# Compression's first layer in native float32 on four column groups of TensorE, with the norm, the values' projection and the small products around it put in another order

## The chip, the cores and the metric

The kernel runs on one NeuronCore of a Trainium2 chip. The metric is the device time of one execution in microseconds (us). Before the change it is 602.39 us, the median of three runs (601.26 to 603.01). A profile of one more execution, of 599.11 us, is what all rows below come from.

## The reference

A decoder trunk of two layers on 256 positions of width 1024, in float32.

- Layer A is an mLSTM mixer: a projection `h @ w_in` to three parts of 2048, a short convolution, gates, a chunkwise cell with four heads, and `y @ w_out` (2048 x 1024). Its result is normed and added to the residual stream `x`.
- From `x`, normed with `kv_norm`, one shared set of keys and values is computed: `kv = rmsnorm(x) @ kv_w`, six parts of 2 groups x 128. Two parts are *compressed*: blocks of 32 positions, 16 apart, get a position vector added, are flattened to 4096 values and go through `silu(flat @ w1 + b1) @ w2 + b2`; `w1` is 4096 x 256, once for keys and once for values (`kv` is 0 or 1 below). Two parts are the keys and values of a selection branch, two those of a window branch.
- Layer B is an attention mixer with 16 heads and three branches (compressed, selected, window) that read these keys and values; it has its own projections (`b_w_in`: queries, 48 branch gates, three sets of silu gates `z`) and ends in `b_w_out`, a norm, and the sum with `x`.

## The kernel before

**How a product is made.** Products are made from two halves of each operand: `hi` is the float32 value rounded to the type float32r, `lo` the rest. `split` (line 123) makes them: ScalarE (ACT) copies `src` into `hi`, VectorE (DVE) writes `lo = src - hi`. `mm3` (line 127) issues three float32r matmuls, hi*hi, hi*lo, lo*hi (lines 129 to 131 of the profile). A weight chunk is 512 KB: `weights` (line 112) issues its DMA on the queue of SyncE (SP) into one of four `raw` buffers and splits it into a ring of five `whi` and four `wlo` buffers. `proj_t` (line 136) makes one projection to 256 output columns: two chunks, 48 matmuls of 256 moving columns. A few small products take plain ("native") float32 operands; the profile shows each of these matmuls as two instructions.

**Order.** The program is traced by a layer that allots buffers, sets the waits, and orders each engine's instructions by a planner: among the instructions that its own clock says are ready it takes the earliest one of the program; `tc.high_priority()` moves instructions forward, and `tc.issue_after(ins)` queues instructions of the same engine behind `ins` without waiting for its end. `held()` does that for the list `hold`. Once made, the order on an engine or a DMA queue is fixed.

**The stretch that the change touches** (about 235 to 340 us of the span):

- `OutProj` (line 186) is layer A's output product, accumulated over 16 row tiles of `w_out`, for two tiles `t` of 128 positions and two column halves `n`. `add` runs row tiles for both `t`; `load_last` keeps the chunks of the last four row tiles (12 to 15), and `finish` runs these for `t=0`, then for `t=1`, and norms each as it ends: squares on ACT (line 161), `u` (163, DVE), a power on GpSimd (POOL, 153), a product with the norm's weights (222), the sum into `x` (224).
- Lines 552 to 574: `x` is normed with `kv_norm` (`norm_t`, line 169: product on DVE, line 175; eight transposes on TensorE (PE), line 178; a split), to `hK`. Four chunks `vch` of value weights are loaded beforehand.
- Lines 638 to 653: the values' projection `vps` for `t=0` and `t=1` (24 matmuls of 512 columns each); then `x` is normed for layer B (`hB`, both `t`).
- Lines 656 to 666: projections `xcps` of the two parts to be compressed; their hi and lo and those of the position vectors go side by side into `XC`, 68 columns per position.
- `cmp_chunk` (line 672): a chunk of `w1`, split; then four float32r matmuls (line 685), 68 stationary columns, 512 moving. Eight chunks for each `kv`, accumulated in `R` (68 x 512).
- `cmp_finish` (line 688): `R` to SBUF, four native matmuls with `comb`, which sums the parts (line 694), bias, tanh, and the second layer (line 706 for keys, 720 for values).
- `branch_gates` (line 733): 24 float32r matmuls with 48 stationary columns, a tanh, two transposes (line 751).
- Lines 896 to 908 set the order: chunks of `w1` with projections (`ks`, `kw`, gates and the first queries, three `z`) between every three chunks, `cmp_finish(0)` after the third chunk of the values, `cmp_finish(1)` last. Then the attention loop (line 917) begins with the scores `sps`.

In layer A the change touches lines 407 to 409 (`ng`, a row of running maxima) and 462 (`dps`, one native matmul per head that spreads a row of `ng` over 128 partitions).

## Time and profile before

| | |
|---|---|
| median of three runs | 602.39 us |
| profiled execution | 599.11 us, of which the span from first to last instruction is 597.3 us |
| PE busy | 580.4 us of the span (97%), granted clock 0.996 of full speed |
| DVE busy | 468.6 us (78%) |
| ACT busy | 330.6 us (55%) |
| DMA moved | 96.67 MB, mean 162 GB/s |

An engine's busy time counts its instructions; matmuls are pipelined, so the step from one matmul's start to the next, and not the duration of one, is what a matmul costs a busy PE. "PEld" is PE's loading of stationary columns. A row of a timeline gives start, duration, engine, line, operation, output and inputs, form, and how many like instructions were merged; a bracket gives the idle time of the engine before it and whom it waited for.

### The profile page before, as it was taken

Reading aid. Unit: us, or ns where it says so; the run is one execution under the profiler, and the core shown is the slowest. Engines: PE = TensorE matmul, PEld = TensorE weight load, DVE = VectorE, ACT = ScalarE, POOL = GpSimd, SP = SyncE. Lnnn points to the kernel's source line nnn. Section 1 sums busy time; section 2 is a strip of 40 time slices with the busy share of each in tenths; the row PEclk is TensorE's granted clock in tenths of the full one; section 3 lists DMA queues with packets and bytes.
Section 4 is the critical chain, followed back from the end, with each engine's and each line's share of the span. In section 5 each row is a group of like instructions: output and inputs, shape, how many; then the busy total and the mean of one; then the engine's idle time right before and its main releaser. Section 6 shows DMA issues by size and latency. Waiting matters only on the chain.

```text
span 597.3 us, 10623 instructions
## 1 busy us (share of the span) xinstructions
PE 580.4 (97%) x4002; PEld 526.2 (88%) x4002; DVE 468.6 (78%) x952; ACT 330.6 (55%) x604; POOL 91.4 (15%) x106
## 2 busy tenths in 40 slices
PE   8998999999999999899999999999999999999995
PEld 4997987989999888679778999999999999998884
DVE  5789886486888875688667688889898989899663
ACT  5565766445444344475566465747475656575621
POOL 7610000101100210250000021212121212120000
PEclk8999999999999999999999999999999999999999
DMA  9985664252421556637989654546364645354501
GB/s 256 229 261 171 213 215 138 77 171 71 142 89 55 169 180 191 186 109 226 272 261 270 184 152 132 163 123 180 111 182 117 179 114 177 108 177 142 180 32 70
DMA packets 82692, 96.67 MB, mean 162 GB/s; under 512 B 4811, under 2 KB 68449, under 8 KB 82642
## 3 DMA queue, kind: packets, MB, share of 16 engines
q1 hardware_dynamic: 81040, 92.48, 51.0%
q0 software_dynamic: 1600, 3.52, 2.7%
q8 instruction: 31, 0.51, 0.4%
q14 instruction: 19, 0.16, 0.1%
q10 hardware_dynamic: 2, 0.00, 0.0%
HBM read 94.94 MB, written 1.05 MB: 161 GB/s over the span
## 4 chain that ended last, share of the span: by engine, by line
PE 80%; DMA 7%; DVE 7%; ACT 2%; issue 2%; POOL 1%; SPq 0%; DVEq 0%; POOLq 0%; ACTq 0%
PE zps L131 10%; PE zps L129 10%; PE zps L130 10%; PE acc L129 4%; PE acc L130 4%; PE acc L131 4%; DMA raw<-in_a_w_in_dram 2%; DVE wlo L125 2%; PE qps L130 2%; PE qps L129 2%; PE qps L131 2%; PE o L129 2%; DMA raw<-in_cmp_w_dram 2%; PE o L130 2%; PE o L131 2%
## 5 line engine op out<-in xcount | busy, mean ns | idle before, releaser
L125 DVE TENSOR_TENSOR wlo<-raw,whi 128x1024 fp32r<-128x1024 f32 x169 | 204.5, 1220 | 58.2 <-ACT whi L124 17.0
L124 ACT ACTIVATE whi<-raw 128x1024 fp32r<-128x1024 f32 x169 | 176.5, 1054 | 127.6 <-issue 30.2
L129 PE MATMUL zps<-hB_hi,whi 128*128 128x256 f32 x384 | 109.3, 285 | 0.0
L131 PE MATMUL zps<-hB_hi,wlo 128*128 128x256 f32 x384 | 108.7, 283 | 0.0
L130 PE MATMUL zps<-hB_lo,whi 128*128 128x256 f32 x384 | 108.6, 283 | 0.0
L774 POOL TENSOR_SCALAR al<-dist 128x800 f32<-128x800 f32 x16 | 43.5, 2721 | 224.6 <-DVE mx L787 218.4
L129 PEld LDWEIGHTS zps<-hB_hi,whi 128*128 128x128 f32 x384 | 73.5, 191 | 0.2
L130 PEld LDWEIGHTS zps<-hB_lo,whi 128*128 128x128 f32 x384 | 73.6, 192 | 0.1
L131 PEld LDWEIGHTS zps<-hB_hi,wlo 128*128 128x128 f32 x384 | 73.6, 192 | 0.0
L795 ACT ACTIVATE e<-e,nm 128x16 f32<-128x16 f32 (+2 forms) x96 | 37.7, 394 | 12.4 <-DVE nm L790 12.0
L131 PE MATMUL xmps<-hA_hi,wlo 128*128 128x256 f32 x128 | 36.6, 286 | 3.0 <-DVE wlo L125 2.9
L129 PE MATMUL zps<-hA_hi,whi 128*128 128x256 f32 x128 | 36.6, 286 | 0.0
L129 PE MATMUL xmps<-hA_hi,whi 128*128 128x256 f32 x128 | 36.3, 284 | 0.2 <-ACT whi L124 0.2
L131 PE MATMUL zps<-hA_hi,wlo 128*128 128x256 f32 x128 | 36.4, 284 | 0.0
L130 PE MATMUL zps<-hA_lo,whi 128*128 128x256 f32 x128 | 36.3, 284 | 0.0
L130 PE MATMUL xmps<-hA_lo,whi 128*128 128x256 f32 x128 | 36.2, 283 | 0.0
L129 PE MATMUL qps<-hB_hi,whi 128*128 128x256 f32 x128 | 36.2, 283 | 0.0
L130 PE MATMUL qps<-hB_lo,whi 128*128 128x256 f32 x128 | 36.2, 283 | 0.0
L131 PE MATMUL qps<-hB_hi,wlo 128*128 128x256 f32 x128 | 36.2, 283 | 0.0
L131 PEld LDWEIGHTS xmps<-hA_hi,wlo 128*128 128x128 f32 x128 | 24.5, 192 | 3.9 <-DVE wlo L125 3.9
L129 PE MATMUL acc<-whi,yhi 128*128 128x512 f32 x64 | 25.6, 399 | 0.0
L130 PE MATMUL acc<-wlo,yhi 128*128 128x512 f32 x64 | 25.4, 397 | 0.0
(328 smaller groups left out, 1438.1 us busy)
## 6 DMA issues: line engine op xcount, KB each, us to landing
raw<-in_b_w_in_dram SPq DMA_DIRECT2D x64, 512.0 KB, 4.7
raw<-in_a_w_in_dram SPq DMA_DIRECT2D x48, 512.0 KB, 4.5
raw<-in_a_w_out_dram SPq DMA_DIRECT2D x16, 512.0 KB, 4.2
raw<-in_cmp_w_dram SPq DMA_DIRECT2D x32, 256.0 KB, 4.4
raw<-in_b_w_out_dram SPq DMA_DIRECT2D x16, 512.0 KB, 3.9
raw<-in_kv_w_dram SPq DMA_DIRECT2D x8, 512.0 KB, 5.5
raw<-in_kv_w_dram SPq DMA_DIRECT2D x8, 256.0 KB, 4.3
x<-in_x_dram SPq DMA_DIRECT2D x4, 256.0 KB, 3.8
```

Source lines behind the costliest of these rows:

```text
L124: a = nc.scalar.activation(hi, src, AF.Copy)
L125: return a.ins, nc.vector.tensor_sub(lo, src, hi.bitcast(F32)).ins
L129: nc.tensor.matmul(dst, lhsT=l[0], rhs=r[0], start=start, stop=False)
L130: nc.tensor.matmul(dst, lhsT=l[0], rhs=r[1], start=False, stop=False)
L131: last_mm[0] = nc.tensor.matmul(dst, lhsT=l[1], rhs=r[0], start=False, stop=stop).ins
L774: nc.gpsimd.tensor_scalar(al, dist, -slopes[h], None, op0=ALU.mult)
L795: nc.scalar.activation(e[:, c0:c0 + n], e[:, c0:c0 + n], AF.Exp, bias=nm[:, i:i + 1], accum_out=sm[:, i:i + 1])
```

## The change

- `finish` runs the matmuls of both `t` first and norms afterwards; layer A's last part has six row tiles in place of four. The chunks of the added two row tiles are split into four of the large `h8` buffers ("homes"), not into the ring.
- The norm for `hK` is traced at high priority and queued on PE behind a matmul three before the end of the output product. The values' projection of each `t` comes right behind its norm, and the norm for `hB` behind that.
- The first layer of the compression is native: `XC` is plain float32 with the position vectors added, 32 columns for each half `a` of a block, and the chunk of `w1` is used as loaded. A chunk is four native matmuls of 32 stationary and 256 moving columns, each into another quarter of the 128 rows of `R`. `w1` has nine buffers of its own (six, and three that take the place of the value weights); nine chunks are asked for while `XC` is made, the others one by one as chunks are used.
- `cmp_finish` is cut in two: `cmp_hidden` (two native matmuls) and the rest; both are queued behind the last matmul of a projection. The list of calls is written out anew.
- The branch gates' hi and lo stand side by side (96 columns): 16 matmuls in place of 24, and two native matmuls in place of the transposes, before the tanh.
- `dps` becomes one float32r matmul of 36 rows, on a hi and lo of `ng` that DVE makes.

```diff
-    def weights(src, a):
+    def weights(src, a, home=None):
...
-        hi = wp.tile([P, 1024], F32R, tag="whi", bufs=5, name=f"whi{n}")
-        lo = wp.tile([P, 1024], F32R, tag="wlo", name=f"wlo{n}")
+        if home is not None:
+            hi, lo = home[:, 0, :], home[:, 1, :]
+        else:
...
         def one(self, t, n, k, wt):
...
+                if kk == 0:
+                    self.near_end = last_mm[0]
...
-        def load_last(self, k0):
-            self.last = [(n, k, self.load(n, k)) for n in range(2) for k in range(k0, self.nk, 2)]
+        def load_last(self, k0, spare=0):
+            homes = [[hp.tile([P, 2, 1024], F32R, tag="h8", name=f"wl{n}{k}") for n in range(2)] for k in range(0, spare, 2)]
+            self.last = [(n, k, self.load(n, k, homes[(k - k0) // 2][n] if k < k0 + spare else None))
+                         for k in range(k0, self.nk, 2) for n in range(2)]
+            self.last.sort(key=lambda e: e[0])
...
             for t in range(NT):
                 for n, k, wt in self.last:
                     self.one(t, n, k, wt)
+            for t in range(NT):
                 with tc.high_priority(), held():
...
+        ng2 = ap.tile([36, S], F32R, name="ng2")
+        pick2 = ap.tile([36, AH], F32R, name="pick2")
+        for t in (ng2, pick2):
+            nc.vector.memset(t.bitcast(F32), 0.0)
+        for r in (0, 32):
+            nc.vector.tensor_copy(pick2[r:r + AH], ident[r:r + AH, r:r + AH])
...
+        nc.vector.tensor_copy(ng2[0:AH], ng)
+        nc.vector.tensor_sub(ng2[32:32 + AH], ng, ng2[0:AH].bitcast(F32))
...
-            nc.tensor.matmul(dps, lhsT=ident[0:AH, h:h + 1].to_broadcast([AH, P]), rhs=ng, start=True, stop=True)
+            nc.tensor.matmul(dps, lhsT=pick2[:, h:h + 1].to_broadcast([36, P]), rhs=ng2, start=True, stop=True)
...
-        op.add(4, (AH - 1) * HT)
-        op.load_last((AH - 1) * HT)
+        op.add(4, (AH - 1) * HT - 2)
+        op.load_last((AH - 1) * HT - 2, 2)
...
-            ins = norm_t(t, rB[t], gam_k, hK)
+            with tc.high_priority(), tc.issue_after(op.near_end):
+                ins = norm_t(t, rB[t], gam_k, hK)
...
+            vps.append(pjt([P, 512], f"vps{t}"))
+            if t == 0:
+                op_end = last_mm[0]
+            with tc.issue_after(op_end):
+                for c in range(4):
+                    for k in range(2):
+                        kk = 2 * c + k
+                        mm3(vps[t], [a[:, kk, t * P:(t + 1) * P] for a in hK], [a[:, k, :] for a in vch[c]],
+                            kk == 0, kk == KT - 1)
+            if t == 0:
+                hB = new_hT("hB")
+            with tc.issue_after(last_mm[0]):
+                norm_t(t, rB[t], gam_b, hB)
...
-        comb = kp.tile([68, 2, BG, NB], F32, name="comb")
+        comb = kp.tile([P, BG, NB], F32, name="comb")
...
+        w1p = [cctx.enter_context(tc.tile_pool(name="w1p", bufs=6, reuse_waits="tile"))]
+        w1t = []
+        def load_w1(eng):
+            i = len(w1t)
+            kv, c = divmod(i, 8)
+            src = cmp_w1[kv].rearrange("(a l p) n -> p l a n", a=2, p=P)
+            raw = w1p[i % 9 // 6].tile([P, 2, 2, 256], F32, tag="w1", name=f"w1_{i}")
+            for l in range(2):
+                eng.dma_start(out=raw[:, l], in_=src[:, 2 * c + l])
+            w1t.append(raw)
...
-        b2 = bctx.enter_context(tc.tile_pool(name="b2", bufs=2, side="right", reuse_waits="tile"))
-        pp = bctx.enter_context(tc.tile_pool(name="pp", bufs=7, side="right", reuse_waits="tile"))
-        hB = new_hT("hB")
-        for t in range(NT):
-            norm_t(t, rB[t], gam_b, hB)
+        qz = bctx.enter_context(tc.tile_pool(name="qz", bufs=2, side="right", reuse_waits="tile"))
+        w1p.append(cctx.enter_context(tc.tile_pool(name="w1q", bufs=3, side="right", reuse_waits="tile")))
...
             hold.clear()
-            X = kp.tile([P, 16, 68], F32R, tag=f"XC{kv}", name=f"XC{kv}")
+            for _ in range((6, 3)[kv]):
+                load_w1(nc.sync)
+            X = kp.tile([P, 2, 16, 32], F32, tag=f"XC{kv}", name=f"XC{kv}")
             psv = ps.rearrange("p g (c l) -> p g c l", l=16)
-            xh, xl = (X[:, :, o:o + 32].rearrange("p l (g c) -> p g c l", g=BG) for o in (0, 32))
-            split(xh, xl, psv)
-            pos = cvec[:, kv * 32:(kv + 1) * 32].rearrange("p (a l) -> p l a", a=2)
-            split(X[:, :, 64:66], X[:, :, 66:68], pos)
+            for a in range(2):
+                pos = cvec[:, kv * 32 + a * 16:kv * 32 + (a + 1) * 16]
+                nc.vector.tensor_add(X[:, a].rearrange("p l (g c) -> p g c l", g=BG), psv,
+                                     pos[:, None, None, :].to_broadcast([P, BG, 16, 16]))
...
         def cmp_chunk(kv, c, R):
...
-            split(hi, lo, raw)
-            for l in range(2):
-                for i, w in enumerate((hi, lo)):
-                    nc.tensor.matmul(R, lhsT=XC[kv][:, 2 * c + l, :], rhs=w[:, l * 512:(l + 1) * 512],
-                                     start=c == 0 and l == 0 and i == 0, stop=c == 7 and l == 1 and i == 1)
+            raw = w1t[kv * 8 + c]
+            for l in range(2):
+                for a in range(2):
+                    r = 32 * (2 * l + a)
+                    nc.tensor.matmul(R[r:r + 32, :], lhsT=XC[kv][:, a, 2 * c + l, :], rhs=raw[:, l, a, :],
+                                     start=c == 0, stop=c == 7)
+            if len(w1t) < 16:
+                load_w1(nc.sync)
+
+        def cmp_hidden(kv, R):
+            rs = tp.tile([P, 256], F32, tag="tmp", name="rs")
+            nc.scalar.activation(rs, R, AF.Copy)
             ps = wkt([P, 2, BG * NB], "hidps")
+            with tc.issue_after(last_mm[0]):
+                for ht in range(2):
+                    nc.tensor.matmul(ps[:, ht, :], lhsT=rs[:, ht * P:(ht + 1) * P],
+                                     rhs=comb.rearrange("p g n -> p (g n)"), start=True, stop=True)
...
             for k in range(KT):
-                mm3(ps, [a[:, k * NGL:(k + 1) * NGL] for a in (hi, lo)], [a[:, k, :] for a in hB], k == 0, k == KT - 1)
-            gT = tp.tile([NGL, S], F32, tag="tmp", name="gT")
-            nc.scalar.activation(gT, ps, AF.Tanh, scale=0.5)
+                for i in range(2):
+                    nc.tensor.matmul(ps, lhsT=hl[:, k].rearrange("p i c -> p (i c)"), rhs=hB[i][:, k, :],
+                                     start=k + i == 0, stop=k + i == KT)
+            gT = tp.tile([2 * NGL, S], F32, tag="tmp", name="gT")
+            nc.scalar.activation(gT, ps, AF.Copy)
...
             for t in range(NT):
-                nc.tensor.transpose(gps[:, t, :], gT[:, t * P:(t + 1) * P], ident[0:NGL, 0:NGL])
-            nc.vector.tensor_scalar(gs, gps, 1.0, 0.25, op0=ALU.add, op1=ALU.mult)
+                nc.tensor.matmul(gps[:, t, :], lhsT=gT[:, t * P:(t + 1) * P], rhs=both_parts, start=True, stop=True)
+            nc.scalar.activation(gs, gps, AF.Tanh, scale=0.5)
+            nc.vector.tensor_scalar(gs, gs, 1.0, 0.25, op0=ALU.add, op1=ALU.mult)
...
+        ks()
+        chunks(0, 0, 4)
+        kw()
+        chunks(0, 4, 8)
+        gT = branch_gates()
+        put(q, 0, q_proj, 0)
+        gate_columns(gT)
+        h0 = cmp_hidden(0, Rs[0])
+        chunks(1, 0, 3)
+        z0[0]()
+        cmp_finish(0, *h0)
+        chunks(1, 3, 8)
+        z0[1]()
+        h1 = cmp_hidden(1, Rs[1])
+        z0[2]()
+        cmp_finish(1, *h1)
         cctx.close()
+        b2 = bctx.enter_context(tc.tile_pool(name="b2", bufs=2, side="right", reuse_waits="tile"))
+        pp = bctx.enter_context(tc.tile_pool(name="pp", bufs=7, side="right", reuse_waits="tile"))
```

The silu gates and the queries move from the pools `pp` and `b2` to `qz`; `chunks(kv, c0, c1)` calls `cmp_chunk` for these chunks.

## Rows read from the trace of the kernel before

**Rows 1.** The profile's page: busy time of the engines over the span, share and number of instructions; and the splits of weight chunks, count, busy time, mean ns of one, and idle time before them.

```profile
PE 580.4 (97%) x4002; PEld 526.2 (88%) x4002; DVE 468.6 (78%) x952; ACT 330.6 (55%) x604; POOL 91.4 (15%) x106
...
L125 DVE TENSOR_TENSOR wlo<-raw,whi 128x1024 fp32r<-128x1024 f32 x169 | 204.5, 1220 | 58.2 <-ACT whi L124 17.0
L124 ACT ACTIVATE whi<-raw 128x1024 fp32r<-128x1024 f32 x169 | 176.5, 1054 | 127.6 <-issue 30.2
```

**Rows 2.** Busy time in stretches of 10 us: length, then busy time (instructions) of each engine, granted clock, mean busy share of the DMA engines, GB/s.

```profile
260.00:270.00 10.00, 10.00 (x70) 9.10 (x69) 9.65 (x15) 6.42 (x11) 4.76 (x2) 1.00 0.34 107
...
280.00:290.00 10.00, 10.00 (x73) 8.83 (x71) 6.24 (x7) 5.12 (x6) 0.00 (x0) 1.00 0.91 283
```

**Rows 3.** Timeline of PE: the end of layer A's output product, the norm for `hK` and the values' projection, up to the first `xcps`.

```profile
246.79 0.40 PE L131 MATMUL acc<-whi,ylo 128*128 128x512 f32 x1
248.88 0.66 PE L178 MATMUL nT<-ident,nrm 128*128 128x128 f32 x4 [1.70 <-DVE nrm L175]
...
250.57 0.40 PE L129 MATMUL vps<-wvhi,hK_hi 128*128 128x512 f32 x1
...
255.84 0.39 PE L131 MATMUL vps<-wvhi,hK_lo 128*128 128x512 f32 x1
256.96 1.29 PE L178 MATMUL nT<-ident,nrm 128*128 128x128 f32 x8 [0.74 <-DVE nrm L175]
258.28 0.50 PE L129 MATMUL vps<-wvhi,hK_hi 128*128 128x512 f32 x1
...
264.29 1.91 PE L178 MATMUL nT<-ident,nrm 128*128 128x128 f32 x16
265.95 0.36 PE L129 MATMUL xcps<-hK_hi,whi 128*128 128x256 f32 x1
```

**Rows 4.** Timeline of PE: the first three chunks of the first layer (line 685, 12 matmuls from 277.55) and the projection behind them; then the two places with a wait for `wlo`.

```profile
277.55 0.40 PE L685 MATMUL R<-whi,XC 128*68 128x512 f32 x1
...
280.30 0.28 PE L129 MATMUL ksps<-hK_hi,whi 128*128 128x256 f32 x1
...
290.97 0.38 PE L131 MATMUL kwps<-hK_hi,wlo 128*128 128x256 f32 x1 [0.32 <-DVE wlo L125]
...
299.03 0.39 PE L685 MATMUL R<-whi,XC 128*68 128x512 f32 x1
300.19 0.45 PE L685 MATMUL R<-wlo,XC 128*68 128x512 f32 x1 [0.77 <-DVE wlo L125]
```

**Rows 5.** Timeline of PE in layer A: the gates' product `gps` (line 377), 32 native matmuls of 32 stationary and 256 moving columns on the four quarters in turn, shown as 64 instructions (first and last two groups), with what stands behind; and eight instructions (four native matmuls of 256 columns) on the whole array, line 472, up to the next group.

```profile
86.71 0.64 PE L377 MATMUL gps<-xm,wgt 128*32 128x256 f32 x8
...
89.33 0.61 PE L377 MATMUL gps<-xm,wgt 128*32 128x256 f32 x8
89.76 0.61 PE L377 MATMUL gps<-xc,wgt 128*32 128x256 f32 x8
90.30 0.39 PE L129 MATMUL zps<-hA_hi,whi 128*128 128x256 f32 x1
...
138.70 0.69 PE L462 MATMUL dps<-ng,ident 4*128 4x256 f32 x2
139.32 1.99 PE L472 MATMUL sps<-xc,kk 128*128 128x256 f32 x8
141.15 1.05 PE L474 MATMUL sps<-xc,kk 128*128 128x128 f32 x8
```

**Rows 6.** Timeline of PE: branch gates (24 matmuls from 300.93), the gates' transposes, the small product behind the first layer, and the second layer of the keys.

```profile
300.93 0.28 PE L129 MATMUL bgps<-hB_hi,whi 128*48 128x256 f32 x1
...
303.93 0.28 PE L129 MATMUL qps<-hB_hi,whi 128*128 128x256 f32 x1
...
309.76 0.32 PE L751 MATMUL gTps<-ident,gT 48*128 48x48 f32 x2
310.01 1.08 PE L694 MATMUL hidps<-comb,rs 68*128 68x32 f32 x8
310.92 0.43 PE L685 MATMUL R<-whi,XC 128*68 128x512 f32 x1
...
314.56 0.28 PE L130 MATMUL zps<-hB_lo,whi 128*128 128x256 f32 x1
316.31 0.63 PE L706 MATMUL kcps<-hid,w 128*128 128x32 f32 x4 [1.48 <-DVE hid L703]
...
339.09 0.37 PE L129 MATMUL sps<-KThi,qhi 128*128 128x272 f32 x1
```

**Rows 7.** Layer A: DVE's chain at `ng`, and PE's transposes of `grows` behind it.

```profile
98.92 0.28 DVE L409 TENSOR_SCALAR ng<-ng 4x256 f32<-4x256 f32 x1
99.24 0.41 DVE L411 TENSOR_TENSOR grows<-ng,grows 4x256 f32<-4x256 f32 x1
...
99.86 0.58 PE L420 MATMUL tps<-ident,grows 4*128 4x4 f32 x4
```

**Rows 8.** Queues: SP's issues of weights before and behind the norm (start, time from the first to the end of the last of so many issues); two issues of POOL, of which the first is of line 914 (through the helper in line 65) and the second of line 588.

```profile
237.92 6.61 SPq L116 DMA_DIRECT2D raw<-in_kv_w_dram  x4
262.10 8.18 SPq L679 DMA_DIRECT2D raw<-in_cmp_w_dram  x6
...
255.99 0.62 POOL L65 DMA_DIRECT2D gam_o<-in_norm_post_dram  x1
256.61 0.55 POOL L588 DMA_DIRECT2D crows<-in_cmp_pos_dram  x1
```

More of the change, by code (lines that the diff above doesn't have):

```diff
@@ L116, in weights @@
         nc.sync.dma_start(out=raw.rearrange("p (a b) -> p a b", a=a), in_=src)
-        hi = wp.tile([P, 1024], F32R, tag="whi", bufs=5, name=f"whi{n}")
-        lo = wp.tile([P, 1024], F32R, tag="wlo", name=f"wlo{n}")
+        if home is not None:
+            hi, lo = home[:, 0, :], home[:, 1, :]
+        else:
+            hi = wp.tile([P, 1024], F32R, tag="whi", bufs=5, name=f"whi{n}")
+            lo = wp.tile([P, 1024], F32R, tag="wlo", name=f"wlo{n}")
         with held():
@@ L192, in __init__, with load @@
             self.acc = [[(wkt if t + n == 2 else pjt)([P, 512], f"acc{t}{n}") for n in range(2)] for t in range(NT)]
-        def load(self, n, k):
-            return weights(self.w[k * P:(k + 2) * P, n * 512:(n + 1) * 512].rearrange("(k p) n -> p k n", p=P), 2)
+        def load(self, n, k, home=None):
+            return weights(self.w[k * P:(k + 2) * P, n * 512:(n + 1) * 512].rearrange("(k p) n -> p k n", p=P), 2, home)
         def one(self, t, n, k, wt):
@@ L565, in trunk @@
         hK = new_hT("hK")
-        rB = []
+        rB, vps = [], []
         for t, n in op.finish():
@@ L639, in trunk @@
         for t in range(NT):
-            ps = pjt([P, 2, BG * DK], f"vps{t}")
-            for c in range(4):
-                for k in range(2):
-                    kk = 2 * c + k
-                    mm3(ps.rearrange("p a b -> p (a b)"), [a[:, kk, t * P:(t + 1) * P] for a in hK],
-                        [a[:, k, :] for a in vch[c]], kk == 0, kk == KT - 1)
-            split(V[t][0], V[t][1], ps)
-        vctx.close()
-        b2 = bctx.enter_context(tc.tile_pool(name="b2", bufs=2, side="right", reuse_waits="tile"))
@@ L701, in cmp_finish @@
             nc.scalar.activation(th, hid, AF.Tanh, scale=0.5)
+            return hid, th
+        def cmp_finish(kv, hid, th):
             if kv == 0:
@@ L704, in cmp_finish @@
                 kps = wkt([P, BG * NB], "kcps")
-                for ht in range(2):
-                    nc.tensor.matmul(kps, lhsT=w2[:, 0, ht, :], rhs=hid[:, ht, :], start=ht == 0, stop=ht == 1)
+                with tc.issue_after(last_mm[0]):
+                    for ht in range(2):
+                        nc.tensor.matmul(kps, lhsT=w2[:, 0, ht, :], rhs=hid[:, ht, :], start=ht == 0, stop=ht == 1)
                 kc = kp.tile([P, BG, NB], F32, name="kc")
@@ L719, in cmp_finish @@
                                                        op0=ALU.add, op1=ALU.mult)
-                        nc.tensor.matmul(vps[:, g, :], lhsT=l.rearrange("p r n -> p (r n)"), rhs=w2[:, 1, ht, :], start=ht == 0, stop=ht == 1)
+                        with tc.issue_after(last_mm[0]):
+                            nc.tensor.matmul(vps[:, g, :], lhsT=l.rearrange("p r n -> p (r n)"), rhs=w2[:, 1, ht, :], start=ht == 0, stop=ht == 1)
                 vcf = tp.tile([6 * NB, BG, DK], F32, tag="tmp", name="vcf")
@@ L737, in branch_gates @@
                               in_=bw[:, NQK:NQK + NGL].rearrange("(k p) c -> p k c", p=P))
[L738 to L741 removed]
+            hl = wp.tile([P, 1024], F32R, tag="whi", bufs=5, name=f"whi{n}")[:, 0:2 * KT * NGL].rearrange(
+                "p (k i c) -> p k i c", k=KT, i=2)
+            split(hl[:, :, 0, :], hl[:, :, 1, :], raw.rearrange("p (k c) -> p k c", k=KT))
+            ps = pjt([2 * NGL, S], "bgps")
             for k in range(KT):
[L743 to L746 removed]
+                for i in range(2):
[3 more added lines that the diff above has]
+            nc.scalar.activation(gT, ps, AF.Copy)
+            return gT
+        both_parts = bp.tile([2 * NGL, NGL], F32, name="both_parts")
+        nc.gpsimd.tensor_add(both_parts, ident[0:2 * NGL, 0:NGL], ident[0:2 * NGL, NGL:2 * NGL])
         def gate_columns(gT):
@@ L759, in q_proj @@
             ps = proj_t(bw, p * 256, hB, "qps")
-            q = [b2.tile([P, 2, S], F32R, tag=f"q{s}", name=f"q{s}{p}") for s in ("hi", "lo")]
+            q = [qz.tile([P, 2, S], F32R, tag=f"q{s}", name=f"q{s}{p}") for s in ("hi", "lo")]
             sc = float(DK) ** -0.5
```

58 lines of the change are left out of this document (14 added, 44 removed).

## The prediction

> **What bounds the kernel now.** I read the page first: PE is busy 97% of the span, no other engine over 78% [rows 1]. So I ask what the change takes from PE's path, matmul by matmul, and what makes PE wait in its place. I then read PE's timeline by steps from one start to the next, and set each excess over the usual step down as a wait. In layer A's end PE stands still twice, for the norm's chain [rows 3]. Behind it the first layer of the compression runs at its own step, with short waits for `wlo`, which DVE makes [rows 4]. One longer wait is the keys' second layer, queued inside a projection before its input is there [rows 6]. Last I read the stretches for DVE and DMA, the candidates for a new bound: DVE is full (9.65 of 10 us) while the norms run, with DMA at 0.34; later DMA is at 0.91 and 283 GB/s [rows 2].
>
> **The first layer.** Now 12 matmuls take 280.30 - 277.55 = 2.75 us, 0.229 each, so 64 take 14.7 us [rows 4]. After: 16 chunks of four native matmuls of 32 x 256. The gates' product in layer A has just this form: eight instructions, that is four matmuls on four quarters, step by 0.43 us (89.33 to 89.76) [rows 5]. 16 x 0.43 = 6.9 us: **-7.8**. The full-array row, eight instructions in 141.15 - 139.32 = 1.83 us, is the other bound: 64 matmuls at 0.46 would be 29.3 us, **+14.6**. I take 0.43, since form, types and order over the quarters are the same; the far end is a rival.
>
> Leaving such a burst costs 0.54 - 0.43 = 0.1 us [rows 5]; with as much for entering, four bursts cost **+0.8**, between 0 and 1.6. The Trainium skill, page "TensorEngine Tiling (Array Packing)", section Tiling Modes, says that changing the tiling mode drains the TensorE. The row agrees that a change costs something, and shows that it is small.
>
> The 16 splits go (1.22 us of DVE and 1.05 of ACT each [rows 1], 20 and 17 us). Both engines are off the path, so that alone gives nothing on PE; it gives the waits for `wlo`: 300.19 - 299.03 - 0.23 = 0.93 in the chunks and 0.32 in `kwps` [rows 4]: **-1.25**, between 0 and -1.6. In place of two splits of `xcps` per part come two DVE additions, hidden by the next projections; without that cover they would cost about as much as the splits that they replace. POOL's `comb` has fewer pieces, and is long done.
>
> **Small products.** Gates: 24 matmuls take 3.00 us, 0.125 each; 16 take 2.0: **-1.0**. The two transposes cost 0.25; two native matmuls are four instructions, at hidden's 0.91/8 = 0.11 about 0.46: **+0.2**. The hidden product goes from eight instructions to four, twice: 2 x 0.91/2, **-0.9**. The keys' second layer waits 316.31 - 314.56 - 0.12 = 1.6 us for `hid`; after, three chunks and a whole projection lie in between: **-1.6** [rows 6]. Tanh and scaling of the gates on ACT and DVE are hidden until the first softmax needs them.
>
> **The norm's stretch.** PE loses 2.09 - 0.23 = 1.86 us before the first transposes of `hK`, 1.12 - 0.23 = 0.89 before the second ones, 0.5 inside these (8 in 1.32 us, where 16 later take 1.66), and 0.5 in the second `vps` (6.01 us; the first took 5.5) [rows 3]: 3.7 us. After, `t=1` runs 36 matmuls instead of 24 while `t=0` is normed: 12 x 0.23 = 2.8 us more cover than the 1.86 that is short. For the second gap, eight transposes of `hB` (0.83 us) lie in the queue ahead. But these need a product on DVE, between the chain's own DVE steps, and DVE is full there [rows 2]. Bounds: 0, if DVE delays the chain by what the order gains, and -3.7. I take **-2.8**, nearer to the rows of PE, since the larger gap has a margin of 0.9 us. What is late next is the split of the first `xcps` chunk. The homes of the two added row tiles lie in buffers that layer A's projections left long before, so they wait for nothing; the DMAs are as many as before.
>
> **`dps`.** Two instructions take 139.32 - 138.70 = 0.62 us, four times [rows 5]. One float32r matmul of 256 columns steps by 0.12 to 0.2: 4 x 0.47, **-1.9**; bounds -1.6 and -2.0. DVE gets a copy and a subtraction on four rows, like those of 0.28 and 0.41 us, ahead of the step that ACT and then PE's transposes `tps` wait for [rows 7]; the memsets can run earlier. If nothing stands ready ahead of `tps` on PE, this costs up to 0.7: **+0.4**, between 0 and 0.8.
>
> **Loads.** A 512 KB chunk takes 0.524 MB / 283 GB/s = 1.85 us [rows 2]. From the end of the output product to the scores, 28 such chunks are needed (16 of `w1`, 4 for `ks` and `kw`, 8 for the queries and three `z`): 52 us. That stretch is 339.09 - 250.57 = 88.5 us now [rows 3, 6] and some 74 after, so DMA suffices on average. It is better used: SP issued nothing between 244.5 and 262.1 [rows 8], and six buffers of `w1` come free when the output product ends. Some loads may still come late (the three buffers in the place of the value weights; the loads 9 to 15, each behind its chunk). Bounds 0 and two loads late, 3.7; I take **+0.85**, nearer to the waits that rows show today.
>
> **Sum.** -7.8 + 0.8 - 1.25 - 1.0 + 0.2 - 0.9 - 1.6 - 2.8 - 1.9 + 0.4 + 0.85 = **-15.0 us**. Against the profiled execution, 599.11, that is 584.1. That execution lies 3.3 us under the median of 602.39, and a measurement will give a median: **587.4 us**. Nothing behind the scores changes but the place of some buffers.
>
> **Rivals.**
> *Loads in the program's order* (slower). If SP's queue keeps the order in which the code asks, four loads of `w1`, the first waiting for the first chunk, stand ahead of `kw`'s weights. From that chunk's end: four loads and one of `kw`, 5 x 1.85, and its split, 1.05 + 1.22, are 11.5 us, less three chunks of 0.43: PE waits 10.2. Then three loads and the first of the queries, 7.4 us (the gates' small one left out), and a split, less 1.3: another 8.4. Together 18.6: 606.0. It turns slower once loads cost 15 us. For it: a queue's order is fixed, and SP stood still once for 17 us. Against: POOL's queue sent a load of line 914 ahead of one of line 588 [rows 8], so what is ready goes first. 0.06.
> *Quarters that overlap less*, the change not doing what it says. At 0.46 each, 29.3 - 6.9 = 22.4 more: 609.8. With an overlap of three a chunk takes 1.83 / 3 = 0.61 us, 16 x 0.18 = 2.9 more: 590.3. The Trainium skill, page "TensorE: Matmul & The Clock Gate", section "Measured speedup vs the span model", gives 3.07 times for four row tiles, by an estimate 0.60 us a chunk. Against both: 64 instructions in 3.59 us, and 1.83 / 0.43 = 4.3 times [rows 5]. 0.04, nearly all for the milder form.
> *DVE holds the norm*: the -2.8 is not there, and the first `xcps` waits for its split, 1.2 us: 591.4. For it: 9.65 of 10 us busy [rows 2]. Against: PE's larger gap lacks 1.86 us of cover and gets 2.8 [rows 3]. 0.15.
> *Late loads*: 3.7 and a split of 2.3 in place of 0.85: 592.5. For it: 0.91 of DMA [rows 2]. Against: the longer lead. 0.10.
>
> **How the numbers follow.** My forecast has 0.65. With every term at its good end (-7.8, 0, -1.6, -1.0, +0.2, -0.9, -1.6, -3.7, -2.0, 0, 0) the sum is -18.4, 584.0; runs spread by 1.1 us under their median and some waits are perhaps longer than I count, so the range begins at 581.5. At the other end the two faster rivals together give 596.5; I stop at 595. About 0.1 is left above (loads in order, both rivals at once, serial quarters) and 0.07 below. Within 0.3% (1.8 us, about what a measurement can tell from no change) lies only a mixture of losses of 13 to 17 us: 0.02. Slower is most of the first rival and the serial quarters: 0.06. Faster: 0.92.
>
> **What would show it.** Right: `R` in bursts of 16 to 20 matmuls, 0.43 us per chunk, some 8 us of PE fewer; DVE with 16 splits fewer; no idle PE before the transposes of `hK`; `kcps` without a wait; `dps` one instruction each; scores starting near 324. Wrong: PE waiting for `whi` or `wlo` of `kwps`, `bgps` or `qps`, with SP's queue waiting for a matmul of line `R` (loads in order); a chunk above 0.6 us; `xcps` waiting for DVE; or a stretch from the scores to the end longer than today's 258 us, which I did not count at all.

## The result and the profile after

The kernel takes **585.23 us** (median of four runs, 584.39 to 585.7) against 601.83 (four runs, 600.24 to 603.01): ratio 0.973, 95% interval 0.971 to 0.976. The forecast was 587.4, in a range of 581.5 to 595.0. The profiled execution took 585.10 us, span 583.3; before, 599.11 and 597.3.

First the page after: busy time of the engines, and the splits of weight chunks.

```profile
PE 571.7 (98%) x4048; PEld 520.5 (89%) x4048; DVE 450.0 (77%) x942; ACT 311.4 (53%) x585; POOL 89.5 (15%) x103
...
L128 DVE TENSOR_TENSOR wlo<-raw,whi 128x1024 fp32r<-128x1024 f32 x150 | 181.4, 1221 | 61.3 <-PE zps L134 22.1
L127 ACT ACTIVATE whi<-raw 128x1024 fp32r<-128x1024 f32 x151 | 157.2, 1053 | 122.1 <-issue 26.4
```

Against [rows 1], DVE and ACT each lose 19 us of work, and that is more than the span lost; yet only 14 us of span went, because PE bounds, before and after. So the comparison goes by PE's landmarks, the first start of a group. PE starts the projections of layer A at 16.4 us after and at 14.5 before, with the same work ahead of it; over the 13 kernels profiled below and here this start lies between 13.8 and 16.5 us. It is a spread between executions. From the gates' product `gps` on, stretches in which nothing was changed repeat within 0.3 us over these kernels, most of them within 0.05, so I count from there; a difference under 0.3 us in one stretch says nothing by itself.

| from, to (us) | before | after | difference |
|---|---|---|---|
| `gps` to first `acc` (with `dps`) | 115.26 | 114.25 | -1.01 |
| `acc` to `vps` | 48.60 | 46.80 | -1.80 |
| `vps` to `xcps` | 15.38 | 14.78 | -0.60 |
| `xcps` to scores (first layer, gates) | 73.14 | 58.60 | -14.54 |
| scores to last `acc` | 251.46 | 254.11 | +2.65 |
| whole | 503.84 | 488.54 | **-15.30** |

In the profile after, `gps` starts at 87.99, the first `acc` at 202.24, the scores at 322.42 and the last `acc` at 576.53 us.

The stretch from the scores on isn't a loss, though it is longer. Before, 164 matmuls of `zps` ran ahead of the scores, 20 of them of the next part; after, 144 do. The 20, at 0.12 us, are 2.4 us that moved behind the scores. So the last of the prediction's signs of being wrong, a stretch from the scores to the end longer than 258 us, is there (260.9), but as moved work; the stretch ahead of the scores is shorter by the same 2.4.

The norm's stretch (compare [rows 3]):

```profile
247.47 1.03 PE L181 MATMUL nT<-ident,nrm 128*128 128x128 f32 x8
...
248.81 0.39 PE L134 MATMUL acc<-whi,ylo 128*128 128x512 f32 x1
249.04 0.40 PE L132 MATMUL vps<-wvhi,hK_hi 128*128 128x512 f32 x1
...
254.60 2.33 PE L181 MATMUL nT<-ident,nrm 128*128 128x128 f32 x15
...
257.80 0.50 PE L134 MATMUL vps<-wvhi,hK_lo 128*128 128x512 f32 x1 [0.21 <-DVE hK_lo L128]
...
263.82 0.37 PE L132 MATMUL xcps<-hK_hi,whi 128*128 128x256 f32 x1
```

No transpose has a bracket now; the eight of `t=0` lie inside layer A's last products, those of `t=1` run with seven of `hB` in one row of 15. Of PE's waits in the whole stretch, 0.21 us is left.

The first layer and the small products (compare [rows 4, 6]), the last three of four bursts of `R`, each with the group behind it, the small products between, and the scores:

```profile
289.09 1.93 PE L712 MATMUL R<-w,XC 128*32 128x256 f32 x32
290.95 0.36 PE L778 MATMUL bgps<-hB_hi,whi 128*96 128x256 f32 x1
...
292.91 0.28 PE L132 MATMUL qps<-hB_hi,whi 128*128 128x256 f32 x1
...
299.03 0.60 PE L723 MATMUL hidps<-comb,rs 128*128 128x32 f32 x4
299.56 1.50 PE L712 MATMUL R<-w,XC 128*32 128x256 f32 x24
300.99 0.38 PE L132 MATMUL zps<-hB_hi,whi 128*128 128x256 f32 x1
...
306.84 0.53 PE L739 MATMUL kcps<-hid,w 128*128 128x32 f32 x4
307.29 2.37 PE L712 MATMUL R<-w,XC 128*32 128x256 f32 x40
309.59 0.39 PE L132 MATMUL zps<-hB_hi,whi 128*128 128x256 f32 x1
...
322.42 0.37 PE L132 MATMUL sps<-KThi,qhi 128*128 128x272 f32 x1
```

The four bursts last 1.87, 1.86, 1.43 and 2.30 us (four, four, three, five chunks), 7.46 in all: 0.435 for a chunk more, and 0.13 for entering and leaving. Gates took 1.96 us, the hidden product 0.53, and `kcps` starts with no wait.

SP's queue after (compare [rows 8]) holds what one rival was about:

```profile
249.23 6.75 SPq L677 DMA_DIRECT2D w<-in_cmp_w_dram  x12
261.46 0.37 SPq L116 DMA_DIRECT2D raw<-in_kv_w_dram  x1
261.93 3.01 SPq L677 DMA_DIRECT2D w<-in_cmp_w_dram  x6
265.04 4.14 SPq L116 DMA_DIRECT2D raw<-in_kv_w_dram  x3
270.09 0.48 SPq L770 DMA_DIRECT2D raw<-in_b_w_in_dram  x1
...
281.97 5.70 SPq L677 DMA_DIRECT2D w<-in_cmp_w_dram  x8
```

Nine chunks of `w1` (two issues each) go out early, and the weights of `ks`, `kw`, gates and queries stand *ahead* of the loads that wait for a chunk to be used. The program asks for them behind. The two stretches of [rows 2], after:

```profile
260.00:270.00 10.00, 10.00 (x74) 9.45 (x73) 7.99 (x11) 4.27 (x6) 0.00 (x0) 1.00 0.92 289
...
280.00:290.00 10.00, 10.00 (x112) 8.46 (x114) 5.29 (x7) 4.67 (x6) 0.00 (x0) 1.00 0.97 290
```

In the first, DVE falls from 9.65 to 7.99 us and DMA rises from 107 to 289 GB/s: the loads now use the time in which SP had stood still.

### The profile page after: what moved, and what is told of

Its sections match the earlier page's. It is cut to its first block, busy times and chain, and to the rows that moved or that the text cites. A ratio compares the mean times of both kernels' runs of the same rounds, so it can differ in the third digit from the quotient of the medians.

```text
span 583.3 us, 10621 instructions
## 1 busy us (share of the span) xinstructions
PE 571.7 (98%) x4048; PEld 520.5 (89%) x4048; DVE 450.0 (77%) x942; ACT 311.4 (53%) x585; POOL 89.5 (15%) x103
## 4 chain that ended last, share of the span: by engine, by line
PE 94%; DVE 3%; issue 1%; ACT 1%; POOL 0%; DVEq 0%; POOLq 0%; ACTq 0%
PE zps L132 11%; PE zps L134 11%; PE zps L133 11%; PE acc L132 5%; PE acc L134 5%; PE acc L133 5%; PE qps L133 3%; PE qps L132 3%; PE qps L134 3%; PE o L132 2%; PE o L133 2%; PE o L134 2%; PE xmps L134 2%; PE xmps L133 2%; PE xmps L132 2%; PE pt L860 2%
## 5 line engine op out<-in xcount | busy, mean ns | idle before, releaser
L128 DVE TENSOR_TENSOR wlo<-raw,whi 128x1024 fp32r<-128x1024 f32 x150 | 181.4, 1221 | 61.3 <-PE zps L134 22.1
L127 ACT ACTIVATE whi<-raw 128x1024 fp32r<-128x1024 f32 x151 | 157.2, 1053 | 122.1 <-issue 26.4
L132 PE MATMUL o<-whi,hA_hi 128*128 128x512 f32 x64 | 25.3, 396 | 0.0
L132 PEld LDWEIGHTS xmps<-hA_hi,whi 128*128 128x128 f32 x128 | 24.5, 192 | 0.9 <-ACT whi L127 0.6
```

What stands on the lines that cost most here:

```text
L127: a = nc.scalar.activation(hi, src, AF.Copy)
L128: return a.ins, nc.vector.tensor_sub(lo, src, hi.bitcast(F32)).ins
L132: nc.tensor.matmul(dst, lhsT=l[0], rhs=r[0], start=start, stop=False)
```

## The experiments

Times are medians; "shift" is the difference to the profile after from `gps` to the last `acc`, which leaves the start out. All edits are to the changed kernel unless said.

**The start.** The kernel before, unchanged, for a second profile.

> The kernel before, unchanged, profiled once more. The two profiles at hand differ at their start: the first xmps matmul stands at 14.45 us before and at 16.38 us after, though the change has nothing there. Theory (the start's spread): the first xmps of this second profile lies anywhere from 14 to 17 us, and from the first xmps to the first scores sps it repeats the 324.6 us of the first profile within 1.5 us. Rival (the change moves the start, by the memsets of ng2 and pick2 and by another instruction stream): 14.45 us again within 0.2.

That execution took 1456.85 us, with PE busy for 1445.9 of it: an outlier that says nothing of the start. The spread of the start is read from the other profiles instead.

**1. Quarters one at a time.** In each burst all chunks of one column group, then those of the next.

```diff
-            for c in range(c0, c1):
-                cmp_chunk(kv, c, Rs[kv])
+            for quarter in range(4):
+                for c in range(c0, c1):
+                    cmp_chunk(kv, c, Rs[kv], quarter)
```

> The kernel after, but within a burst of chunks the matmuls of one quarter of R follow each other (all chunks for quarter 0, then 1, 2, 3); same matmuls, same result, same loads. Theory (quarters run beside each other only when successive matmuls lie in different quarters): a native matmul on its own steps by 0.43 to 0.46 us, so 64 take 27.5 to 29.3 us instead of 7.4, and the kernel is 20 to 22 us longer, 605 to 607 us. Rival (the 32-column form is cheap by itself, whatever the order): within 1.5 us of 585.2. Between: overlap only at the changes of quarter, 64 - 16 steps of 0.43 and little else, still 15 us longer or more.

595.54 us (594.58 to 596.52), shift +10.7, all of it in `R`: 18.09 us in place of 7.46. Neither size was met. The bursts, PE's timeline:

```profile
305.53 2.87 PE L711 MATMUL R<-w,XC 128*32 128x256 f32 x24
308.33 0.39 PE L132 MATMUL zps<-hB_hi,whi 128*128 128x256 f32 x1
...
314.63 6.32 PE L711 MATMUL R<-w,XC 128*32 128x256 f32 x40
320.88 0.38 PE L132 MATMUL zps<-hB_hi,whi 128*128 128x256 f32 x1
```

Twelve matmuls took 2.80 us, 16 took 4.52 twice, 20 took 6.25. That is 0.43 for each one more. My mean of 0.28, on which I built the next expectation, was the wrong reading: the bursts aren't proportional to their length, they are 0.43 per matmul less a fixed 2.4 us, which is what the three changes of group in a burst overlap. The starts of the single instructions agree: the 40 of the last burst fall into four series at 0.216 us an instruction, and each series begins 1.33 us behind the start of the one before. Ten instructions need 2.16 us, so each series overlaps the one before by 0.83.

**2. Two groups in turn.** One pair of groups for all chunks of a burst, then the other pair.

```diff
+            for half in range(2):
+                for c in range(c0, c1):
+                    for quarter in (2 * half, 2 * half + 1):
+                        cmp_chunk(kv, c, Rs[kv], quarter)
```

> As the changed kernel, but in each burst the matmuls alternate between two of the four column groups, first one pair for all its chunks, then the other. In the run with one group at a time a matmul took 0.28 us, with four in turn 0.11. Theory (each group takes 0.28 us for its own matmul and groups overlap whole): 0.14 us per matmul, 2.3 us for a burst of 16 and 9.2 us for all 64, 587 us. Rival A (two neighbours don't overlap, or only in part): 0.2 to 0.28 us, 13 to 18 us in all, 591 to 595. Rival B (two groups are enough and something else sets 0.11): 7.5 us, 585.2.

588.86 us (two runs), shift +3.8; `R` took 11.02 us, between the theory's 9.2 and rival A's 13.

```profile
301.36 1.96 PE L711 MATMUL R<-w,XC 128*32 128x256 f32 x24
303.25 0.39 PE L132 MATMUL zps<-hB_hi,whi 128*128 128x256 f32 x1
...
309.56 3.68 PE L711 MATMUL R<-w,XC 128*32 128x256 f32 x40
313.18 0.39 PE L132 MATMUL zps<-hB_hi,whi 128*128 128x256 f32 x1
```

1.89, 2.76 and 3.62 us for 12, 16 and 20 matmuls: 0.216 for each one more. With one group in turn it is 0.43, with two 0.216, with four 0.109. So the theory's mechanism holds, at 0.43 and not at 0.28: a group needs 0.43 us for its matmul, and groups that alternate overlap whole. The Trainium skill, page "TensorEngine Tiling (Array Packing)", section Tiling Modes, says that different tiles can execute in parallel; these three steps agree.

**3. The native layer alone.** The kernel *before* with the native first layer, its weights through the four `raw` buffers that all weights share, and nothing else of the change.

```diff
-            hi = wp.tile([P, 1024], F32R, tag="whi", ...)
-            lo = wp.tile([P, 1024], F32R, tag="wlo", ...)
-            split(hi, lo, raw)
...
-                    nc.tensor.matmul(R, lhsT=XC[kv][:, 2 * c + l, :], rhs=w[:, l * 512:(l + 1) * 512], ...)
+                    r = 32 * (2 * l + a)
+                    nc.tensor.matmul(R[r:r + 32, :], lhsT=XC[kv][:, a, 2 * c + l, :], rhs=rv[:, l, a, :], ...)
```

> The kernel before with the native first layer on four quarters alone: chunks in the four raw buffers, used as loaded, the old order of calls, four-tile end, old values, gates and dps. Theory (the first layer's own PE time is most of the gain): chunks fall from 14.7 to 7.4 us, the hidden product by 0.9, and the wait for wlo in the chunks goes: 8.5 to 9.5 us less than before, 592.3 to 593.3 us. Rival (the buffers of w1 are needed: a raw buffer is now held until its matmuls, so loads come later): new waits of PE for DMA of 2 to 6 us in the stretch of the chunks, 594 to 599 us.

611.39 us (608.85 to 613.67) against 600.01 of the kernel before: 1.9% longer (ratio 1.019, 1.015 to 1.022), and outside both ranges. PE waited 4.6 us for `w1` and 3.8 for the splits of `kw` and the gates; the granted clock was 0.83 in 290 to 310 us.

**4. The shared buffers in the new order.** That run also had the old order of chunks and projections. So the changed kernel, in its order, with `w1` through the four `raw` buffers:

```diff
-            raw = w1p[i % 9 // 6].tile([P, 2, 2, 256], F32, tag="w1", ...)
+            raw = wp.tile([P, 1024], F32, tag="raw", ...)
...
-            for _ in range((6, 3)[kv]):
-                load_w1(nc.sync)
```

> As the changed kernel, in its order, but the first layer's weights go through the four buffers that all raw weights share, as in the kernel before, and nothing is loaded ahead. Theory (a native matmul holds its raw buffer until PE is through with it, where a split on ACT and DVE let go of it earlier; so the shared buffers stop the loads of the projections behind them): PE waits 8 to 20 us ahead of chunks and projections, 593 to 605 us. Rival (the slow run with the native layer alone came from chunks and projections being interleaved three by three, not from the buffers): waits under 3 us, 585 to 588.

611.81 us (610.85 to 612.59), shift +26.7: the shared buffers without a lead do it, in the new order too; the loss is larger than I allowed. The waits named add up to 14 us; the granted clock falls to 0.66 behind them, and PE's steps get longer. PE's waits (us in total, times, longest) and one of SP, then a stretch (length, busy time of PE, PEld, DVE, ACT and POOL, granted clock, DMA share, GB/s):

```profile
PE zps L132 <- ACT whi L127: 4.5, 1, 4.5
...
PE kwps L132 <- ACT whi L127: 3.5, 1, 3.5
PE R L710 <- DMA raw<-in_cmp_w_dram: 2.9, 1, 2.9
PE bgps L774 <- DVE whi L128: 2.9, 1, 2.9
```

```profile
SPq L116 <- PE R L710: 19.3, 8, 7.9
```

The row of SP shows the mechanism: SP's issues of the projections' weights (line 116) stood 19.3 us behind matmuls of `R`. In the profiles before and after, no issue of that line waits for `R`. The stretch:

```profile
300.00:310.00 10.00, 8.37 (x44) 8.06 (x45) 3.13 (x4) 3.32 (x6) 0.00 (x0) 0.66 0.96 268
```

**5. A short ring of its own.** Four buffers for `w1` in place of nine, four loads ahead.

```diff
-        w1p = [cctx.enter_context(tc.tile_pool(name="w1p", bufs=6, ...))]
+        w1p = [cctx.enter_context(tc.tile_pool(name="w1p", bufs=4, ...))]
...
-        w1p.append(cctx.enter_context(tc.tile_pool(name="w1q", bufs=3, ...)))
...
-            for _ in range((6, 3)[kv]):
+            for _ in range((4, 0)[kv]):
```

> As the changed kernel, but the first layer's weights have four buffers in place of nine, and only four chunks are issued ahead of the compression's projections; the next is issued when a chunk has been used, as the other loads are. Theory A (the lead of the loads is what the new buffers bring, and without it the native chunks wait, as in the run with the native layer alone, where two waits were 3.0 and 2.8 us): chunks 4 to 15 wait, 3 to 8 us in all, 588 to 593 us. Theory B (the chunks spread behind projections give enough time, and in the native layer alone it was the planner's interleaving that cost): 585.2 +- 1 us, bursts of 7.5 us in all.

588.03 us (586.83 to 589.21), shift +3.7, at the lower end of theory A's range: the second burst took 293.18 - 289.45 = 3.73 us in place of 1.86, `R` 10.01 in all. That is 2.6 us more, a little under the 3 to 8 that theory A named; another 0.9 lies in `zps`, between whose matmuls the last chunks came singly. PE's timeline:

```profile
289.45 3.80 PE L711 MATMUL R<-w,XC 128*32 128x256 f32 x32
293.18 0.36 PE L777 MATMUL bgps<-hB_hi,whi 128*96 128x256 f32 x1
```

So a lead of four chunks in place of nine costs under 4 of run 4's 26.7 us; the rest is left for the ring that the projections' weights share, and for loading nothing ahead. These two were not tried apart.

**6. Loads in the program's order.** The weights of `ks`, `kw`, the gates and the first queries are issued behind the loads of `w1` that the program has ahead of them.

```diff
-        kw()
+        with tc.issue_after(last_ld[0]):
+            kw()
```

(and the same for `ks`, and for the gates with the queries)

> As the changed kernel, but the weights of ks, kw, the gates and the first q projection are issued on SP only after the loads of the first layer's weights that stand ahead of them in the program: nine chunks ahead of ks, four more ahead of kw, the rest ahead of the gates. In the profile after, the planner had put the weights of kw, the gates and part of q ahead of the last seven chunks. Theory (that order is why PE waits for no load there): a chunk is 512 KB, 1.6 us at the 323 GB/s of that stretch, so ks comes about 3 x 1.6 = 5 us later than its need, kw and the gates up to 7 x 1.6 = 11 us: 590 to 600 us, and the profile shows PE waits of 1 us and more ahead of ksps, kwps or bgps. Rival (the buffers for raw weights lead by enough to cover it): 585.2 +- 1 us and no wait over 0.3 us ahead of those projections.

598.14 us (596.44 to 600.56), shift +14.2, in the theory's range. Its wait came ahead of `kw` alone: ahead of `ks` and the gates' product PE waited for no load. SP's queue, then PE's timeline, then one stretch:

```profile
283.52 3.95 SPq L678 DMA_DIRECT2D w<-in_cmp_w_dram  x8
287.56 1.37 SPq L116 DMA_DIRECT2D raw<-in_kv_w_dram  x2
```

```profile
296.19 0.58 PE L132 MATMUL kwps<-hK_hi,whi 128*128 128x256 f32 x1 [9.71 <-ACT whi L127]
...
299.11 0.41 PE L132 MATMUL kwps<-hK_hi,whi 128*128 128x256 f32 x1
299.32 0.41 PE L133 MATMUL kwps<-hK_lo,whi 128*128 128x256 f32 x1
```

```profile
290.00:300.00 10.00, 3.35 (x14) 3.05 (x15) 2.45 (x2) 2.11 (x2) 0.00 (x0) 0.50 1.10 334
```

The weights of `kw` went out at 287.56 in place of 265.04, behind the loads that wait for the first burst, and PE stood for 9.71 us, close to the 10.2 that the prediction's rival gave for this wait. That rival's second wait, 8.4 us ahead of the queries, did not come. Behind the wait a matmul stepped by 0.21 us where it takes 0.12: the granted clock is 0.50 in this stretch, the lower of the two levels (1.2 GHz), after PE had stood still. From the first `kwps` to `bgps` it is 9.42 us, in the profile after 5.95 without the burst that lies there: 3.5 us more, of which 0.5 is a second wait and the rest the clock.

**7. Small products at once.** Hidden product and second layer right behind the chunks, no forced order.

```diff
-        h0 = cmp_hidden(0, Rs[0])
         chunks(1, 0, 3)
+        cmp_finish(0, *cmp_hidden(0, Rs[0]))
```

(and the same for the second compression; the three `tc.issue_after(last_mm[0])` around these small products go)

> As the changed kernel, but the second layer of the compression follows its hidden product at once, right behind the chunks, with nothing issued between and no order forced. Theory (the wait of 1.63 us ahead of kcps was the chain hidden product, addition, tanh, product on DVE and ACT, and placing projections between took it away): the wait of about 1.6 us comes back for the first compression, and one of the same chain ahead of the second's values product, where no projection is left to cover it: +1.6 to +3.2 us, 586.8 to 588.4. Rival (the planner moves the small products back by itself, or fills the wait with matmuls that are ready): +0 to +0.5 us.

587.49 us (586.2 to 589.1), shift +1.7: the theory's lower end.

```profile
303.62 0.63 PE L739 MATMUL kcps<-hid,w 128*128 128x32 f32 x4 [1.55 <-DVE hid L735]
```

The first wait is back. In place of the second, the planner ran 21 `zps` of the next part ahead of the scores, as the kernel before did: `ksps` to scores is 4.43 us longer, scores to the end 2.73 shorter.

**8. Four row tiles at the end.**

```diff
-        op.add(4, (AH - 1) * HT - 2)
-        op.load_last((AH - 1) * HT - 2, 2)
+        op.add(4, (AH - 1) * HT)
+        op.load_last((AH - 1) * HT)
```

> The kernel after, with four row tiles in the last part of the output product as before, the rest as changed. Theory (the two added row tiles give the cover for the norm of t=0): PE stands still again before the first transposes of hK, by 1.2 to 2.0 us; 586.4 to 587.4 us. Rival (the order with high priority and near_end gives the gain): no idle time of PE there beyond 0.3 us, within 0.4 us of 585.2.

588.0 us (586.92 to 588.77), shift +3.5, all of it between `acc` and `vps`; more than the theory's 1.2 to 2.0, of its sign. PE's timeline, the first transposes and the first `vps`; then the same stretch in this run and in the kernel before:

```profile
250.18 0.85 PE L181 MATMUL nT<-ident,nrm 128*128 128x128 f32 x4 [2.19 <-DVE nrm L178]
...
252.97 0.63 PE L132 MATMUL vps<-wvhi,hK_hi 128*128 128x512 f32 x1
```

```profile
245.00:255.00 10.00, 7.81 (x31) 6.14 (x30) 7.74 (x15) 4.01 (x10) 4.41 (x10) 0.83 0.42 126
```

```profile
245.00:255.00 10.00, 8.30 (x41) 6.44 (x40) 6.86 (x12) 5.27 (x14) 4.69 (x12) 1.00 0.36 105
```

The wait explains some 2 us, and the granted clock behind it, 0.83, the rest. From the first transposes to the first `vps` eleven matmuls take 252.97 - 250.18 = 2.79 us here and 250.57 - 248.88 = 1.69 in the kernel before [rows 3], at a clock of 1.00; with the next three `vps`, 1.13 us where the kernel before takes 0.72, the clock cost about 1.5 us of this execution. Without it the shift would be some 2.0, the theory's upper end. Two of the other executions took 586.92 and 587.31 us at a mean clock of 0.999 and 0.998, in the theory's range; the third took 588.77 at 0.997. In run 3 a wait of 2.13 us at the same place left the clock at 1.00.

**9. Values behind both norms.** The values' projection of both `t` after both `t` of the first norm, as before.

```diff
-            with tc.high_priority(), tc.issue_after(op.near_end):
-                ins = norm_t(t, rB[t], gam_k, hK)
+            ins = norm_t(t, rB[t], gam_k, hK)
...
+        for t in range(NT):
             for c in range(4):
...
+        hB = new_hT("hB")
+        for t in range(NT):
+            norm_t(t, rB[t], gam_b, hB)
```

> As the changed kernel, but the values' projection of both row tiles and the second norm's transposes come after both row tiles of the first norm, as in the kernel before; six row tiles still end the first layer. Theory (values behind their own norm cover the transposes' wait for the other row tile's norm): a wait of 0.5 to 2.5 us returns between the last product of the first layer and the values, 585.7 to 587.7. Rival (the planner runs what is ready whatever the program's order): within 0.5 us of 585.2.

592.33 us (590.46 to 594.21), shift +7.5, three times what the theory allowed. Up to `xcps` it was +1.1; most of the rest, 4.3 of 6.1 us, stands in one row, PE's timeline, with POOL's issue:

```profile
270.37 0.25 PE L626 MATMUL cvps<-ident,crows 70*128 70x70 f32 x1 [4.30 <-DMA crows<-in_cmp_b_dram]
```

```profile
263.12 0.56 POOL L617 DMA_DIRECT2D crows<-in_cmp_pos_dram  x1 [9.14 <-PE nT L181]
```

`crows` uses one of the two buffers of the norms' `nrm`. In this order it came free with the last transposes, and the load was issued at 263.12; in the profile after, at 258.14. So the same run with a buffer of its own for it:

```diff
-        crows = tp.tile([70, P], F32, tag="tmp", name="crows")
+        crows = kp.tile([70, P], F32, name="crows")
```

> As the run with the values behind both row tiles, but the rows of the compression's biases and positions (crows) have a buffer of their own, in place of one of the two that the norms use, so that their load does not stand behind the last norm's transposes. In the run before it, that load was issued on POOL at 263.1 us in place of 258.1, and PE waited 4.3 us for it. Theory (the values behind their own norm are worth the two waits of 0.89 and 1.26 us ahead of the transposes, less what the order forced by the change costs, 1.1 us net by the start of xcps; the rest was the buffer): the wait of 4.3 is gone, first xcps 1.1 us later than in the profile after once both are set to the same start of the first layer's acc, and the run 586 to 587.5 us. Rival (the order brings the rest in another way, the gates' and ks' loads being later): 589 us and more.

587.28 us (586.33 to 587.98), shift +1.4. The wait is gone, `acc` to `xcps` is 1.6 us longer than after, where the theory said 1.1. The theory holds; the rest was the buffer: in the run before this, 4.3 us of wait, and behind it a granted clock of 0.83 in 270 to 280, where the profile after has 1.00.

**10. `dps` native.**

```diff
-            nc.tensor.matmul(dps, lhsT=pick2[:, h:h + 1].to_broadcast([36, P]), rhs=ng2, ...)
+            nc.tensor.matmul(dps, lhsT=ident[0:AH, h:h + 1].to_broadcast([AH, P]), rhs=ng, ...)
```

> As the changed kernel, but the broadcast of -g over 128 partitions is one native float32 matmul of 256 columns per head again. Theory (by the profiles, 0.62 us before against 0.31 after, four heads): +1.27 us, 586.5. Rival (the work beside it sets the pace, and the step is hidden): 585.2 +- 0.3. By the prediction's own term: +1.9, 587.1.

586.37 us (585.44 to 587.02), shift +1.4, in the stretch `gps` to `acc` (+1.37). The two forms in PE's timeline, first the profile after, then this run:

```profile
108.60 0.38 PE L480 MATMUL dps<-ng,pick 36*128 36x256 f32 x1
108.91 1.35 PE L490 MATMUL sps<-xc,kk 128*128 128x256 f32 x5
```

```profile
109.10 0.69 PE L480 MATMUL dps<-ng,ident 4*128 4x256 f32 x2
109.73 0.48 PE L490 MATMUL sps<-xc,kk 128*128 128x256 f32 x1
```

## Why the prediction was right

| step | forecast | measured | by |
|---|---|---|---|
| first layer, entry and exit, waits for `wlo` | -8.25 | -8.9 | bursts of `R`, 15.96 to 7.46; `kwps`, 6.32 to 5.95 |
| gates; their transposes | -1.0, +0.2 | -1.04, +0.13 | timeline |
| hidden product, twice | -0.9 | -0.83 | timeline |
| `kcps` wait | -1.6 | -1.63 | timeline, run 7 (+1.7) |
| norm's stretch | -2.8 | -2.40 | `acc` to `xcps` |
| `dps`, four | -1.9 | -1.24 | timeline, run 10 (+1.37) |
| DVE's steps ahead of `tps` | +0.4 | +0.16 | `tps` to `kkps` |
| late loads | +0.85 | 0 | no wait for a load |
| sum | -15.0 | -15.7 | the table of stretches: -15.30 |

The 0.4 between the two sums is spread over groups that the change doesn't touch, and is within what stretches differ by. That the forecast's sum lies so near is partly luck: `dps` and the norm's stretch gave 1.1 us less than their terms, while the late loads that did not come, the first layer and the steps ahead of `tps` gave 1.7 more. The gates and the hidden product were read from the timeline and not tried alone.

**The first layer** went by the row that I chose: the four native matmuls of a chunk step together by 0.435 us, forecast 0.43. The choice of the gates' product, same form and same alternation, was what made the term right; runs 1 and 2 show that alternation is the condition, since one group at a time cost 10.6 us more in `R`, and the term gained 8.5. The rival of quarters that overlap less is out: 0.435 us a chunk is not 0.61.

**The loads.** The mechanism of the rival is real and was put at about the right price for its first wait (9.71 us, forecast 10.2), while its second wait did not come; and the planner's order isn't the program's, as I argued from POOL's queue. What I under-rated is what the nine new buffers carry. I weighed them as a lead for the loads, with a loss of 3.7 us at worst; without a ring of their own and the lead the change is 26.7 us slower (run 4), and at 611.81 us slower than the kernel before. I had no rival for that, and none was needed, as the change has the ring.

**The norm's stretch** gained 2.40 of the 2.8. The two parts don't add. From `acc` to `xcps` it is 63.98 us before and 61.58 after. With the row tiles alone (run 9, second form) it is 63.17, a gain of 0.8; with the order alone (run 8) it is 65.01, or by the estimate there 63.5 without the lower clock, a gain of 0.5. So either part alone is worth less than 1 us, and both together 2.4. DVE did not hold the norm.

**The steps ahead of `tps`** cost nothing by the way that I forecast: `tps` starts 13.15 us behind `gps` before and after, with matmuls of `o` ahead of it as cover. The 0.16 us lie behind it, where the planner put a matmul of `o` between the transposes.

**`dps`** is the term that I mis-sized: I let one float32r matmul step by 0.12 to 0.2 us, from rows inside long series. Alone between two native products it steps by 108.91 - 108.60 = 0.31, so the gain is 0.31 per head and not 0.47.

**The base.** The profile lost 14.0 us, the medians 16.6. The start explains 1.3 of the 2.6 (from `gps` on it is 15.3). The rest, 1.3, is that the other executions of the kernel before lay 1.1 to 3.9 us above its profiled one, and those of after within 0.7 of theirs; why is open. The 31 later executions of the kernel before have medians of 600.01, 600.32 and 600.59 in their three series, 14.8 to 15.4 above 585.23, so the 16.6 owes something to a series that lay high. The five of the 31 that took over 602 us have the lowest mean granted clocks, 0.990 or 0.991 (the others 0.992 to 0.999), which points to a clock that falls in some executions and does not prove it. I went from the median, 587.4, which is 2.2 us above 585.23; from the profiled execution it would have been 584.1, 1.1 below.

## What to carry over

Price a matmul of a partly used array by a row of the same form in the same alternation, and a single matmul by a row where it stands alone. Where a weight is no longer split, its raw buffer is held until TensorE is through with it: give it a ring of its own, or the loads queued behind it pay. When an order of norms or chunks is moved, look at every small tile that shares their buffers, and behind a wait of TensorE allow for a lower granted clock: it came behind waits of 2.19, 4.30 and 9.71 us here, and not behind one of 2.13.

## What had not been expected

- Column groups overlap in full proportion: 0.43, 0.216 and 0.109 us per native matmul of 32 x 256 with one, two and four groups in turn, and entering and leaving a burst of four groups costs 0.13 us together.
- A burst that changes its group three times is 2.4 us shorter than its matmuls at 0.43 each, which makes 0.8 us of overlap at each change.
- A wait of 9.71 us of PE was followed by a granted clock of 0.50 and steps of 0.21 us in place of 0.12. In run 8 a wait of 2.19 us was followed by 0.83, which cost about 1.5 us more.
- Three loads of 1 to 32 KB that stood behind a shared buffer stopped PE for 4.3 us.
